# Seven products of quarters for part of the FFN's down projection, and a convolution that reads PSUM

## The chip, the cores and the metric

The kernel runs on one core of a Trainium2 chip. The metric is the device time of one execution in microseconds (us). Before the change the median of three runs is 1321.83 us (1321.08 to 1322.3).

The engines are named as in the profile: PE is TensorE's matmul, PEld its weight load, DVE is VectorE, ACT is ScalarE, POOL is GpSimd, and SP is SyncE, which issues most of the transfers.

## The reference, cut to what matters

The reference is two layers of an encoder on 512 positions of width 1024: a mixer (neighbourhood attention and grouped-query attention), cross attention over 256 memory positions, and a feed-forward network (FFN) with a short convolution. Then a final norm. The change touches the FFN:

```python
def conv_ffn(h, w_up, conv_w, conv_b, w_down):      # D_FF = 2816
    u = h @ w_up                                    # 512 x 1024 by 1024 x 5632
    up = jnp.pad(u, ((0, 0), (1, 1), (0, 0)))
    u = up[:, :-2] * conv_w[0] + up[:, 1:-1] * conv_w[1] + up[:, 2:] * conv_w[2] + conv_b
    gate, val = jnp.split(u, 2, axis=-1)
    return (jax.nn.silu(gate) * val) @ w_down       # 512 x 2816 by 2816 x 1024
```

## The kernel before, in words

**Numbers.** Every float32 operand of a product is split into a part `hi` of type float32r, rounded, and the rest `lo`. A product is then three matmuls, `hi*hi`, `hi*lo` and `lo*hi`, into one PSUM tile (`mm3`, lines 606 to 610). So each operand costs a cast on ACT (`hi`) and a subtraction on DVE or POOL (`lo`). All arrays lie transposed: 128 channels on the partitions, 512 positions along the row. The residual is `xT[0]` to `xT[7]`, one tile for every 128 of the 1024 channels.

**FFN.** D_FF is 22 blocks of 128 channels. For a block `j`, `up_project` (line 1465) makes the gate and the value side, each 8 chunks x 3 = 24 matmuls of 512 columns. `up_finish` (line 1491) multiplies both by the norm's factor `ffn.rep` (DVE, PSUM to an SBUF tile of tag `t`). Then per side ACT makes the middle tap of the convolution, and DVE adds the two outer taps with four `scalar_tensor_tensor`, two of 504 and two of 7 columns (line 1509). Silu, product and split into `hi` and `lo` follow (`acts[j]`, an `rpair`). `down` (line 1517) multiplies a group of blocks by `w_down`: for each of the 8 row blocks `m` of the output one PSUM tile, nj x 3 matmuls of 512 columns, and one DVE addition to `xT[m]`. `GROUPS` holds 8, 7 and 7 blocks. The last group of layer 0 closes the rows for the next norm (`nn.close`). In layer 1 `down_last` (line 1540) computes the first 384 positions as before and the last 128 with the operands swapped, then the final norm and the output.

**Weights.** `weights()` (line 1660) lists the weight blocks in the order of use. `get_w` (line 572) hands out the next one and keeps two more ahead: a DMA into a tile `raw` (`N_RAW` = 2 buffers), a cast on ACT into `hi`, a subtraction on POOL into `lo` (`N_W` = 4 buffers each). A block has up to 1024 columns.

**Order.** Nothing is issued as the code is run. `Tape` records every instruction (hence one line, 393, for nearly all in the profile), and `Tape.plan` orders each engine's list: PE nearly as written, the others by the time at which their results are due. Each engine then works through its own list strictly in order, and semaphores hold it where an operand isn't there. PSUM is eight tiles of 512 columns: 4 of tag `mm`, 2 of `sc`, 2 of `tr` (`ps_mm`, `ps_s`, `ps_t`). In the FFN before, all products go through `mm`.

Of the kernel before, what the change touches and what calls it, by code (L numbers as in the profile page):

```python
# [12 lines left out]
F32R = mybir.dt.float32r  # L13
# [6 lines left out]
P = 128  # L20
S = 512
D = 1024
DEPTH = 2
# [30 lines left out]
MEM_FILL = [1, 1, 2, 2, 1, 3, 1, 3, 1, 3, 1]  # L54
N_ROWS = 3
LATE = 3600
N_RAW, N_W, AHEAD, AHEAD_HELD, N_WARM, N_LATE, N_FIRST = 2, 4, 2, 5, 7, 4, (12, 22)


ENGINES = range(5)  # L60
# [427 lines left out]
def encoder_kernel(ctx: ExitStack, tc: tile.TileContext, t: dict, out: list):  # L488
# [9 lines left out]
    rpool = ctx.enter_context(tc.tile_pool(name="rpool", bufs=21))  # L498
# [24 lines left out]
    def tmp(shape=(S,)):  # L523
        return tpool.tile([P, *shape], F32, tag="t", name=nm("t"))
# [26 lines left out]
    def emit_raw():  # L551
        SP.dma_start(*raw_tile())

    def emit_split(act=ACT, cuts=2):
        n = len(ready)
        key, src, nk, ncol, eng = plan[n]
        raw = raws[n]
        raws[n] = None
        if key[0] in ("up", "down", "memq", "memo"):
# [302 lines left out]
    for l in range(DEPTH):  # L862
# [600 lines left out]
        acts = {}  # L1463

        def up_project(j, side):
            pm = ps_mm()
            gemm_T(pm, get_w(("up", j, side)), ffn.ops, range(KC), 0, KC - 1)
            return pm

        def up_first():  # L1470


            ws, us = [], []
            for side in range(2):
# [7 lines left out]
            us1 = [up_project(1, 0)]  # L1482
            ffn.spread()
            up_finish(0, us)
            us1.append(up_project(1, 1))
            up_finish(1, us1)

        def up(j):
            up_finish(j, [up_project(j, side) for side in range(2)])

        def up_finish(j, us):
            for side in range(2):
                u = tmp()
                DVE.tensor_mul(u, us[side], ffn.rep)
                us[side] = u
            cs = []
            for side in range(2):
                ch = side * NF + j
# [12 lines left out]
            ACT.activation(cs[0], cs[0], AF.Silu)  # L1511
            DVE.tensor_mul(cs[0], cs[0], cs[1])
            acts[j] = rpair()
            ACT.copy(acts[j][0], cs[0])
            DVE.tensor_sub(acts[j][1], cs[0], f(acts[j][0]))

        def down(g):
            j0, nj = GROUPS[g]
# [21 lines left out]
        def down_last(g):  # L1540
# [7 lines left out]
            ws = []  # L1548

            def part(k, c, n):  # L1550
                i, hl = c // 512, ws[3] if k == nj - 1 else ws[k // 2 + 4 * (c // 512)]
                if k == nj - 1:
                    return [w[:, 0, c : c + n] for w in hl]
                return [w[:, k % 2, c - 512 * i : c - 512 * i + n] for w in hl]

            norm = Norm(cols=cs)
            rows = []
            for m in range(KC):
                if m % 4 == 0:
                    ws.extend(get_w(("down", g, n)) for n in range(len(ws), 4 + 3 * (m // 4)))  # L1560
# [59 lines left out]
        for g, (j0, nj) in enumerate(GROUPS):  # L1620
            for j in range(j0 + (g > 0), j0 + nj):
                if j == 0:
                    up_first()
                elif j > 1:
                    up(j)
            if g + 1 < len(GROUPS):
                up(j0 + nj)
            elif l + 1 < DEPTH:
                nn = Norm(G_MIX, l + 1)
            else:  # L1630
                down_last(g)
                break
            down(g)

    tape.play(tc)


# [22 lines left out]
def weights():  # L1660
# [8 lines left out]
    def up(j):  # L1669
        return [cols(("up", j, i), "w_up", 0, KC, i * D_FF + P * j, P) for i in range(2)]  # L1670

    blocks = []
    for l in range(DEPTH):
        for n, p in NA_ORDER:
            if n == "v":
                blocks += wide("v", "w_in", 1024, "DPDP")
            else:
                eng = "Dx" if l == 0 and (n, p) in NA_ORDER[:3] else "P"
                blocks.append(cols((n, p), "w_in", 0, KC, (0 if n == "q" else 512) + P * p, P, eng))
        for kh in range(2):  # L1680
            blocks.append(cols(("gkv", kh), "w_in", 4 * kh, 4, 2048, 256))
        blocks += wide("gq", "w_in", 1536)
        for mp in range(4):
            blocks.append(cols(("outn", mp), "w_out", 0, 4, 256 * mp, 256))
# [11 lines left out]
        for g, (j0, nj) in enumerate(GROUPS):  # L1696
            for j in range(j0 + (g > 0), j0 + nj + (g + 1 < len(GROUPS))):
                blocks += up(j)
            if l + 1 < DEPTH or g + 1 < len(GROUPS):
                blocks += [cols(("down", g, m), "w_down", j0, nj, P * m, P) for m in range(KC)]  # L1700
                continue
            for n, (k0, c0) in enumerate(((0, 0), (2, 0), (4, 0), (6, None), (0, 512), (2, 512), (4, 512))):
                at = (k0, 1, 0, D) if c0 is None else (k0, 2, c0, 512)
                blocks.append(cols(("down", g, n), "w_down", j0 + at[0], *at[1:], "P" if n < 2 else "Pr"))
    return blocks


# [67 lines left out]
```

## Time and profile before

| | |
|---|---|
| median of 3 runs | 1321.83 us |
| the profiled execution: its time | 1320.67 us |
| its span (first to last instruction) | 1318.6 us |
| PE busy | 1311.6 us (99%) |
| DVE / ACT / POOL busy | 939.1 (71%) / 675.6 (51%) / 692.0 us (52%) |
| granted TensorE clock | 1.0 |
| the FFN of layer 0 after its first up block, as one piece of the chain of waits | 315.27 us to 658.11 us |

A busy share counts the time in which the engine has at least one instruction in work. Matmuls overlap: a single one is listed with 390 ns, but the next starts after 227 ns, so times on PE are taken here from start to start. The chain that ended last is followed back from the last instruction; what is on it sets the time. The rows of groups give engine, operation, `out<-in` by tile tags, shape and count, then busy us and mean ns, then the idle time before them.

### The profile page before, as it was taken

To read this page: it belongs to the slowest core of one execution; us is meant where nothing else is said; L and a number is where in the kernel's file an instruction comes from. 1 tells how busy PE (TensorE), PEld (TensorE's weight loads), DVE (VectorE), ACT (ScalarE), POOL (GpSimd) and SP (SyncE) were. 2 spreads that over 40 slices of the span, in tenths; PEclk is the share of its full clock that TensorE was granted. 3 is DMA by queue.
4 is the path that set the end of the run, shared out by engine and by line. 5 is a ranking of instruction groups with operands and counts; after the bars stand their busy time and mean duration, and the time that the engine had idled before them with its cause. 6 is when DMAs were issued, how large, how long until landed. Compare 5 with 4: busy or idle time off the path is not lost.

```text
span 1318.6 us, 17725 instructions
## 1 busy us (share of the span) xinstructions
PE 1311.6 (99%) x6367; PEld 1106.7 (84%) x6367; DVE 939.1 (71%) x1656; ACT 675.6 (51%) x1229; POOL 692.0 (52%) x481
## 2 busy tenths in 40 slices
PE   9999999999999999999999999999999999999998
PEld 8898888888888888888888988888888888888887
DVE  7688886776994488188445898967779835862875
ACT  7786786555442244143447867865644423432432
POOL 3565866726544444444636657765454444444451
PEclk9999999999999999999999999999999999999999
DMA  7752222322333333332355422223133333323331
GB/s 250 208 169 64 82 69 92 96 61 84 112 96 96 97 97 97 102 124 79 101 160 160 145 65 80 69 92 96 49 112 104 99 99 98 92 84 112 96 112 64
DMA packets 42806, 137.28 MB, mean 104 GB/s; under 512 B 5088, under 2 KB 8672, under 8 KB 42720
## 3 DMA queue, kind: packets, MB, share of 16 engines
q1 hardware_dynamic: 42288, 135.83, 33.5%
q8 instruction: 50, 0.82, 0.3%
q10 hardware_dynamic: 432, 0.33, 0.1%
q14 instruction: 36, 0.29, 0.1%
HBM read 126.18 MB, written 2.10 MB: 97 GB/s over the span
## 4 chain that ended last, share of the span: by engine, by line
PE 99%; ACT 0%; DVE 0%; issue 0%; ACTq 0%
PE mm L393 87%; PE sc L393 8%; PE tr L393 4%; ACT t L393 0%; ACT r L393 0%; DVE r L393 0%; DVE s L393 0%; ACTq L393 0%
## 5 line engine op out<-in xcount | busy, mean ns | idle before, releaser
L393 POOL TENSOR_TENSOR lo<-raw,hi 128x1024 fp32r<-128x1024 f32 (+2 forms) x268 | 512.8, 1924 | 490.3 <-ACT hi L393 485.4
L393 PE MATMUL mm<-xg,hi 128*128 128x512 f32 (+1 forms) x1730 | 535.8, 390 | 0.0
L393 ACT CAST hi<-raw 128x512 fp32r<-128x512 f32 (+2 forms) x276 | 226.2, 839 | 355.7 <-PE mm L393 274.7
L393 PEld LDWEIGHTS mm<-xg,hi 128*128 128x128 f32 x1730 | 322.7, 188 | 65.1
L393 PE MATMUL mm<-xg,lo 128*128 128x512 f32 (+1 forms) x865 | 336.8, 389 | 0.0
L393 PE MATMUL mm<-r,hi 128*128 128x512 f32 (+1 forms) x1040 | 326.8, 390 | 0.0
L393 DVE SCALAR_TENSOR_TENSOR t<-t,par,t 128x504 f32<-128x504 f32 (+1 forms) x352 | 286.7, 852 | 38.5 <-ACT t L393 36.5
L393 PEld LDWEIGHTS mm<-r,hi 128*128 128x128 f32 x1040 | 194.4, 188 | 38.6
L393 PE MATMUL mm<-r,lo 128*128 128x512 f32 (+2 forms) x552 | 207.5, 376 | 0.0
L393 PEld LDWEIGHTS mm<-xg,lo 128*128 128x128 f32 x865 | 162.5, 188 | 33.5
L393 PEld LDWEIGHTS mm<-r,lo 128*128 128x128 f32 x552 | 103.7, 188 | 19.3
L393 DVE TENSOR_TENSOR xT<-xT,mm 128x512 f32<-128x512 f32 (+1 forms) x56 | 37.1, 666 | 111.8 <-PE mm L393 111.5
L393 PE MATMUL mm<-hi,xg 128*128 128x512 f32 (+1 forms) x384 | 107.6, 358 | 0.0
L393 POOL TENSOR_SCALAR t<-t,s 128x512 f32<-128x512 f32 (+1 forms) x112 | 66.3, 606 | 65.0 <-DVE s L393 61.2
L393 DVE TENSOR_TENSOR t<-mm,rep 128x512 f32<-128x512 f32 x88 | 60.1, 687 | 36.9 <-PE mm L393 36.8
L393 PE MATMUL sc<-r,r 128*128 128x256 f32 (+1 forms) x382 | 83.5, 336 | 0.0
L393 ACT ACTIVATE t<-t,par 128x512 f32<-128x512 f32 x88 | 71.0, 812 | 18.8 <-DVE t L393 18.8
L393 ACT ACTIVATE t<-sc,s,s 128x512 f32<-128x512 f32 (+1 forms) x96 | 67.9, 711 | 23.7 <-DVE s L393 20.6
L393 PEld LDWEIGHTS mm<-hi,xg 128*128 128x128 f32 x384 | 68.3, 189 | 9.3
L393 PE MATMUL tr<-ident,t 128*128 128x128 f32 x488 | 70.4, 272 | 0.0
L393 PEld LDWEIGHTS tr<-ident,t 128*128 128x128 f32 x488 | 59.3, 140 | 10.8
L393 PE MATMUL mm<-lo,xg 128*128 128x512 f32 (+1 forms) x192 | 68.3, 356 | 0.0
(124 smaller groups left out, 1517.1 us busy)
## 6 DMA issues: line engine op xcount, KB each, us to landing
raw<-in_w SPq DMA_DIRECT2D x192, 512.0 KB, 3.6
raw<-in_w SPq DMA_DIRECT2D x24, 448.0 KB, 3.3
r<-r SPq DMA_DIRECT2D x30, 256.0 KB, 4.0
r<-in_bias SPq DMA_DIRECT2D x16, 384.0 KB, 6.0
r<-in_memT SPq DMA_DIRECT2D x4, 512.0 KB, 7.4
xT<-in_w SPq DMA_DIRECT2D x7, 256.5 KB, 4.2
out<-xT SPq DMA_DIRECT2D x8, 192.0 KB, 2.1
r<-in_w SPq DMA_DIRECT2D x9, 128.0 KB, 3.9
```

The lines of the kernel that those rows point to most:

```text
L393: call(*args, **kwargs)
```

## The change

**Down projection.** Blocks 0 to 15 of D_FF are taken in four groups of four (`GROUPS`), the last six as before. In a group the four blocks are two halves of two. For one pair of row blocks, `m` and `m + 4`, the weights of a group are a 2 x 2 matrix of quarters (rows `m` or `m + 4`, first or second half of the blocks), and the activations are one too (half of the blocks, positions 0 to 255 or 256 to 511). `down_halved` multiplies them by Strassen's scheme in Winograd's form: seven products of quarters for eight, on sums and differences of quarters. Each product has 2 blocks x 3 = 6 matmuls of 256 columns. They go in pairs into the halves of a PSUM tile.

**Sums of weights.** `combined` replaces the split for such a block of 1024 columns: ACT casts 768 and twice 512 columns, DVE subtracts 768, POOL makes four sums of 256 columns and twice subtracts 512. **Sums of activations**: `halved` makes them for two blocks of D_FF at a time. **Order**: `UPS` is the order of the up blocks; from the sixth on, one pair of rows of a group (`BEHIND` = 5) stands behind each up block, in `weights()` and in the loop. **Convolution**: the products of `up_project` go to `sc` and `tr` tiles, the norm's factor is multiplied in place in PSUM, and ACT and DVE read the convolution's input there. `N_RAW` is 3, the pool of `r` tiles has 23 instead of 21 buffers.

The diff, cut:

```diff
-GROUPS = [(0, 8), (8, 7), (15, 7)]
+GROUPS = [(0, 4), (4, 4), (8, 4), (12, 4), (16, 6)]
+UPS = [j0 + i // 2 + nj // 2 * (i % 2) for j0, nj in GROUPS[:-1] for i in range(nj)] + list(range(GROUPS[-1][0], NF))
+BEHIND, ROWS_HALVED = 5, KC // 2 * (len(GROUPS) - 1)
...
+    LO_A, SUMS, LO_S = DVE, POOL, POOL
...
+    def combined(raw):
+        hi, lo = [wpool.tile([P, 6, P], F32R, tag=tag, name=nm(tag)) for tag in ("hi", "lo")]
+        shi, slo = rtile((8, P)), rtile((8, P))
+        a11, a12, a22, a21 = (raw[:, 2 * i : 2 * i + 2] for i in range(4))
+        first, second = tmp((4, P)), tmp((4, P))
+        ACT.copy(hi, raw[:, 0:6])
+        LO_A.tensor_sub(lo, raw[:, 0:6], f(hi))
+        SUMS.tensor_add(first[:, 0:2], a21, a22)
+        SUMS.tensor_sub(first[:, 2:4], a11, a21)
+        SUMS.tensor_sub(second[:, 0:2], first[:, 0:2], a11)
+        SUMS.tensor_sub(second[:, 2:4], a12, second[:, 0:2])
+        for v, c in ((first, slice(0, 4)), (second, slice(4, 8))):
+            ACT.copy(shi[:, c], v)
+            LO_S.tensor_sub(slo[:, c], v, f(shi[:, c]))
...
         def up_project(j, side):
-            pm = ps_mm()
+            pm = ps_t() if side else ps_s()
...
             for side in range(2):
-                u = tmp()
-                DVE.tensor_mul(u, us[side], ffn.rep)
-                us[side] = u
+                DVE.tensor_mul(us[side], us[side], ffn.rep)
...
+        def halved(j, u):
+            n = UPS.index(j)
+            if n % 4 == 0:
+                shared[:] = [rtile((2, 2, H))]
+            if n % 2 == 0:
+                waiting[n + 1] = u
+                hl = shared[0][:, n // 2 % 2]
+                ACT.copy(hl[:, 0], u[:, :H])
+                DVE.tensor_sub(hl[:, 1], u[:, :H], f(hl[:, 0]))
+                return
...
+            DVE.tensor_sub(first[:, 0], a[:, H:], a[:, :H])
+            DVE.tensor_sub(second[:, 0], b[:, 1], first[:, 0])
+            DVE.tensor_sub(first[:, 1], b[:, 1], a[:, H:])
+            DVE.tensor_sub(second[:, 1], b[:, 0], second[:, 0])
+            ACT.copy(bh[:, 0], b)
+            DVE.tensor_sub(bh[:, 1], b, f(bh[:, 0]))
+            for v, c in ((first, slice(0, 2)), (second, slice(2, 4))):
+                ACT.copy(hi[:, c], v)
+                DVE.tensor_sub(lo[:, c], v, f(hi[:, c]))
...
+        def down_halved(g, m):
...
+            def product(pm, a, b):
+                for k, q in enumerate(qs):
+                    mm3(pm, *ws[k // 2][a][k % 2], *q[b], k == 0, k == len(qs) - 1)
...
+            one = pair(("11", "11"), ("s2", "t2"))
+            ACT.copy(u, one[:, :H])
+            DVE.tensor_add(left, left, one[:, :H])
+            DVE.tensor_add(u, one[:, H:], u)
+            two = pair(("12", "21"), ("s4", "22"))
+            DVE.tensor_add(xT[m], xT[m], two)
+            DVE.tensor_add(right, right, u)
+            three = pair(("22", "t4"), ("s1", "t1"))
+            DVE.tensor_add(xT[m + 4], xT[m + 4], three)
+            DVE.tensor_add(right, right, three[:, H:])
+            four = ps_mm()[:, :H]
+            product(four, "s3", "t3")
+            DVE.tensor_add(u, four, u)
+            DVE.tensor_add(below, below, u.unsqueeze(1).to_broadcast([P, 2, H]))
...
+        for n in range(NF):
+            if n == 0:
+                up_first()
+            elif n > 1:
+                up(UPS[n])
+            if 0 <= n - BEHIND < ROWS_HALVED:
+                down_halved(*divmod(n - BEHIND, KC // 2))
```

Two places show the order, each engine's list for itself.

PE, layer 0: before, a row of the down projection in the middle group (`mm_1004` is the PSUM tile of the row, `r_` the activations, `hi_992` and `lo_993` the weights):

```order
L393 MATMUL mm_1000<-r_986,hi_988 128x512 x2
L393 MATMUL mm_1000<-r_986,lo_989 128x512
L393 MATMUL mm_1004<-r_876,hi_992 128x512 x2
L393 MATMUL mm_1004<-r_876,lo_993 128x512
L393 MATMUL mm_1004<-r_921,hi_992 128x512 x2
L393 MATMUL mm_1004<-r_921,lo_993 128x512
L393 MATMUL mm_1004<-r_934,hi_992 128x512 x2
```

PE after the change, layer 0: the last matmul of an up block (tag `tr`, value side), and the first of the rows behind it (`mm_846` holds the products `one`):

```order
L395 MATMUL tr_831<-xg_641,lo_818 128x512
L395 MATMUL mm_846<-r_775,hi_824 128x256 x2
L395 MATMUL mm_846<-r_775,lo_825 128x256
L395 MATMUL mm_846<-r_775,hi_824 128x256 x2
L395 MATMUL mm_846<-r_775,lo_825 128x256
L395 MATMUL mm_846<-r_785,r_826 128x256
```

The matmuls of 512 columns of the down projection have become ones of 256, each with its own weights, and they stand between up blocks instead of in one piece behind a group.

DVE, layer 0, before: one up block (`t_846` and `t_847` are the two sides in SBUF, `t_848` and `t_849` the convolution's sums):

```order
L393 TENSOR_TENSOR t_846<-mm_838,rep_770 128x512
L393 SCALAR_TENSOR_TENSOR t_836<-t_834,par,t_836 128x504
L393 SCALAR_TENSOR_TENSOR t_836<-t_834,par,t_836 128x7
L393 TENSOR_TENSOR t_835<-t_835,t_836 128x512
L393 SCALAR_TENSOR_TENSOR t_848<-t_846,par,t_848 128x504
L393 SCALAR_TENSOR_TENSOR t_848<-t_846,par,t_848 128x7
L393 TENSOR_TENSOR t_847<-mm_842,rep_770 128x512
L393 TENSOR_TENSOR r_837<-t_835,r_837 128x512
```

DVE after the change, layer 0, an up block of the value side (`tr_880`) up to the additions of the next rows (`mm_918` holds their products `one`; `lo_924` is the subtraction of a weight block):

```order
L395 SCALAR_TENSOR_TENSOR t_885<-tr_880,par,t_885 128x7
L395 TENSOR_TENSOR t_884<-t_884,t_885 128x512
L395 TENSOR_TENSOR t_888<-t_884,t_887 128x256
L395 TENSOR_TENSOR t_887<-t_884,t_862 128x256
L395 TENSOR_TENSOR t_888<-t_884,t_888 128x256
L395 TENSOR_TENSOR r_886<-t_884,r_886 128x512
L395 TENSOR_TENSOR lo_924<-raw_906,hi_923 128x768
L395 TENSOR_TENSOR r_890<-t_887,r_889 128x512
L395 TENSOR_TENSOR r_890<-t_888,r_889 128x512
L395 TENSOR_TENSOR xT_79<-xT_79,mm_918 128x256
L395 TENSOR_TENSOR t_917<-mm_918,t_917 128x256
```

The convolution's input is now a PSUM tile, and eight operations with two SBUF inputs stand in one row, ahead of additions that wait for PE.

More of the change, by code (lines that the diff above doesn't have):

```diff
@@ L552, in emit_raw @@
         SP.dma_start(*raw_tile())
+    def combined(raw):
[12 more added lines that the diff above has]
+            LO_S.tensor_sub(slo[:, c], v, f(shi[:, c]))
+        parts = {}
+        for i, n in enumerate(("11", "12", "22")):
+            parts[n] = [(hi[:, 2 * i + k], lo[:, 2 * i + k]) for k in range(2)]
+        for i, n in enumerate(("s1", "s3", "s2", "s4")):
+            parts[n] = [(shi[:, 2 * i + k], slo[:, 2 * i + k]) for k in range(2)]
+        return parts
     def emit_split(act=ACT, cuts=2):
@@ L558, in emit_split @@
         raws[n] = None
+        if eng == "S":
+            ready.append(combined(raw))
+            return
         if key[0] in ("up", "down", "memq", "memo"):
@@ L1512, in up_finish @@
             DVE.tensor_mul(cs[0], cs[0], cs[1])
+            if j < GROUPS[-1][0]:
+                halved(j, cs[0])
+                return
             acts[j] = rpair()
@@ new lines, in down_halved, with pair @@
+        def down_halved(g, m):
+            j0, nj = GROUPS[g]
+            qs = [quads[j] for j in range(j0, j0 + nj // 2)]
+            ws = [get_w(("down", g, m, q)) for q in range(nj // 4)]
+            def product(pm, a, b):
+                for k, q in enumerate(qs):
+                    mm3(pm, *ws[k // 2][a][k % 2], *q[b], k == 0, k == len(qs) - 1)
+            def pair(left, right):
+                pm = ps_mm()
+                product(pm[:, :H], *left)
+                product(pm[:, H:], *right)
+                return pm
+            left, right = (xT[m][:, c] for c in (slice(0, H), slice(H, S)))
+            below = xT[m + 4].rearrange("p (n q) -> p n q", n=2)
+            u = tmp((H,))
+            one = pair(("11", "11"), ("s2", "t2"))
[12 more added lines that the diff above has]
+            DVE.tensor_add(below, below, u.unsqueeze(1).to_broadcast([P, 2, H]))
@@ L1550, in part @@
             def part(k, c, n):
-                i, hl = c // 512, ws[3] if k == nj - 1 else ws[k // 2 + 4 * (c // 512)]
-                if k == nj - 1:
-                    return [w[:, 0, c : c + n] for w in hl]
+                i, hl = c // 512, ws[k // 2 + 3 * (c // 512)]
                 return [w[:, k % 2, c - 512 * i : c - 512 * i + n] for w in hl]
@@ L1559, in down_last @@
                 if m % 4 == 0:
-                    ws.extend(get_w(("down", g, n)) for n in range(len(ws), 4 + 3 * (m // 4)))
+                    ws.extend(get_w(("down", g, n)) for n in range(len(ws), 3 + 3 * (m // 4)))
                 rows.append(ps_mm()[:, :N_COLS])
@@ L1618, in down_last @@
             ACT.dma_start(out[1][:, 640:D], yf[:, 640:])
[L1620 to L1633, printed above, removed]
+        for n in range(NF):
[5 more added lines that the diff above has]
+                down_halved(*divmod(n - BEHIND, KC // 2))
+        if l + 1 < DEPTH:
+            nn = Norm(G_MIX, l + 1)
+            down(len(GROUPS) - 1)
+        else:
+            down_last(len(GROUPS) - 1)
     tape.play(tc)
@@ L1670, in up, with quarters @@
         return [cols(("up", j, i), "w_up", 0, KC, i * D_FF + P * j, P) for i in range(2)]
+    def quarters(key, k0, half, m):
+        k = np.array([k0, k0 + 1])
+        ks = np.concatenate([k, k + half, k + half, k])
+        rows = (ks[:, None] * P + np.arange(P)).T
+        return key, "w_down", l, rows, np.repeat([P * m, P * (m + 4)], 4), P, "S"
     blocks = []
@@ L1695, in weights @@
             blocks.append(cols(("memo", 0, mp), "w_mem_o", 0, 4, 256 * mp, 256))
[L1696 to L1704, printed above, removed]
+        for n in range(NF):
+            blocks += up(UPS[n])
+            if 0 <= n - BEHIND < ROWS_HALVED:
+                g, m = divmod(n - BEHIND, KC // 2)
+                j0, nj = GROUPS[g]
+                blocks += [quarters(("down", g, m, q), j0 + 2 * q, nj // 2, m) for q in range(nj // 4)]
+        g = len(GROUPS) - 1
+        j0, nj = GROUPS[g]
+        if l + 1 < DEPTH:
+            blocks += [cols(("down", g, m), "w_down", j0, nj, P * m, P) for m in range(KC)]
+            continue
+        for n in range(6):
+            blocks.append(cols(("down", g, n), "w_down", j0 + 2 * (n % 3), 2, 512 * (n // 3), 512, "P" if n < 2 else "Pr"))
     return blocks
@@ L1755 @@
     a["w_in"] = a["w_in"][:, :, _in_order()]
-    blocks = [a[name][l, rows][:, :, c0 : c0 + ncol] for _, name, l, rows, c0, ncol, _ in weights()]
+    blocks = [
+        a[name][l, rows][:, :, c0 : c0 + ncol] if np.ndim(c0) == 0 else
+        np.stack([a[name][l, rows[:, i], c : c + ncol] for i, c in enumerate(c0)], axis=1)
+        for _, name, l, rows, c0, ncol, _ in weights()]
     x = np.concatenate([a["x"].reshape(ROWS, GW, D).transpose(2, 1, 0).reshape(D, S), a["norm_mix"][0][:, None]], axis=1)
```

21 lines of the change are left out of this document (16 added, 5 removed).

## The prediction

> **What bounds the kernel now.** I read the page's busy times first, then the chain of waits, then the FFN's stretches by window, and last the groups of DVE and POOL there.
>
> The page's busy times, and its shares of the chain that ended last by engine:
>
> ```profile
> PE 1311.6 (99%) x6367; PEld 1106.7 (84%) x6367; DVE 939.1 (71%) x1656; ACT 675.6 (51%) x1229; POOL 692.0 (52%) x481
> PE 99%; ACT 0%; DVE 0%; issue 0%; ACTq 0%
> ```
>
> The chain of waits in order of time (start, length, what, count):
>
> ```profile
> 94.65 3.36 PE mm L393 x28
> ...
> 315.27 342.84 PE mm L393 x1512
> ...
> 967.26 333.92 PE mm L393 x1512
> ```
>
> PE carries the end, and in the FFN it has no gap at all: one piece of 1512 matmuls in layer 0, another in layer 1. So matmul time taken out of the FFN comes off the end, as long as that piece stays whole. 342.84 us / 1512 = 226.7 ns is what a matmul of 512 columns costs. For 256 and 384 columns the timeline has stretches of one kind (a merged row starts with its first matmul):
>
> ```profile
> 94.97 0.28 PE L393 MATMUL mm<-hi,xg 128*128 128x256 f32 x1
> ...
> 97.73 0.29 PE L393 MATMUL mm<-hi,xg 128*128 128x256 f32 x1
> ...
> 1295.81 5.37 PE L393 MATMUL mm<-r,r 128*128 128x384 f32 x30
> ```
>
> From 94.97 to 97.73 us the timeline holds 23 starts, so 256 columns cost 2.76 / 23 = 120 ns; the chain's 3.36 / 28 says the same. Each of them loads its own weights, as the new products do. For 384 columns the 30 starts end one tail (0.33 us less a pitch) before the row's end: about 174 ns.
>
> **PE: removed and added.** Blocks 0 to 15 cost, in layer 0, 8 rows x 16 x 3 = 384 matmuls of 512 columns. In layer 1 one of the sixteen stood in the last group, so there it is 8 x 15 x 3 = 360 of 512 columns, 24 of 384 and 6 of 512 with swapped operands. Removed: 750 x 226.7 + 24 x 174 = 170.0 + 4.2 = 174.2 us. Added: 2 layers x 16 row pairs x 7 products x 6 = 1344 matmuls, x 120 = 161.3 us. Seven products for eight would take off an eighth, 21 us; as 256 columns cost more than half of 512, 12.9 us stay. All of it lies in the unbroken pieces.
>
> Here a page speaks against the change. The Trainium skill, "TensorE: Matmul & The Clock Gate", section "Back-to-back issue gap", gives streams of weight load and matmul about 131 ns at 512 columns and 81 at 128; on a straight line between, an estimate of 98 at 256, the sum would be a loss of some 31 us. This trace disagrees at both sizes (226.7 and 120 ns), so the rows decide.
>
> **DVE in the FFN.** This is what could break the cover. A stretch of up blocks alone, then one of down rows alone, before (columns: length, then busy us of PE, PEld, DVE, ACT, POOL):
>
> ```profile
> 446.00:518.00 72.00, 72.00 (x319) 59.64 (x318) 59.59 (x78) 30.35 (x40) 31.93 (x14) 1.00 0.30 95
> 403.00:441.00 38.00, 38.00 (x169) 31.50 (x168) 11.11 (x14) 8.45 (x10) 17.26 (x7) 1.00 0.31 96
> ```
>
> An up block is 48 x 226.7 ns = 10.88 us of PE, and DVE is busy 83% of it, 9.00 us; POOL 4.83 us. The down rows, where DVE rests, are now mixed in: a step after the change is an up block and a row pair, 10.88 + 42 x 0.120 = 15.92 us. Its DVE work, from the groups of the FFN of layer 0 (316 to 667 us), and two smaller ones from the whole run:
>
> ```profile
> L393 DVE SCALAR_TENSOR_TENSOR t<-t,par,t 128x504 f32<-128x504 f32 x88 | 117.4, 1339 | 19.6 <-ACT t L393 18.6
> L393 DVE TENSOR_TENSOR t<-mm,rep 128x512 f32<-128x512 f32 x44 | 30.1, 687 | 17.7 <-PE mm L393 17.7
> L393 DVE TENSOR_TENSOR xT<-xT,mm 128x512 f32<-128x512 f32 x16 | 11.0, 688 | 51.6 <-PE mm L393 51.5
> L393 DVE SCALAR_TENSOR_TENSOR xg<-mm,par,xg 128x512 fp32r<-128x512 f32 x8 | 6.0, 748 | 5.1 <-ACT xg L393 5.1
> L393 DVE TENSOR_TENSOR r<-t,r 128x512 fp32r<-128x512 f32 x22 | 26.1, 1184 | 3.0 <-ACT r L393 2.2 <-DMA raw<-in_w 0.7
> ...
> L393 DVE TENSOR_TENSOR t<-mm,r 128x256 f32<-128x256 f32 x16 | 6.0, 420 | 1.3 <-ACT t L393 1.2
> ```
>
> The first and the fifth row stand out: with both inputs in SBUF an operation takes 1339 or 1184 ns, with one in PSUM 748 or 688. The timeline of one up block shows why:
>
> ```profile
> 461.73 0.74 DVE L393 SCALAR_TENSOR_TENSOR t<-t,par,t 128x504 f32<-128x504 f32 x1
> 462.39 0.68 DVE L393 TENSOR_TENSOR t<-mm,rep 128x512 f32<-128x512 f32 x1
> 463.00 0.22 DVE L393 SCALAR_TENSOR_TENSOR t<-t,par,t 128x7 f32<-128x7 f32 x1
> ...
> 469.37 2.47 DVE L393 SCALAR_TENSOR_TENSOR t<-t,par,t 128x504 f32<-128x504 f32 x1 [0.33 <-ACT t L393]
> 471.77 0.68 DVE L393 TENSOR_TENSOR r<-t,r 128x512 fp32r<-128x512 f32 x1
> ```
>
> POOL's row of that moment:
>
> ```profile
> 468.70 2.60 POOL L393 TENSOR_TENSOR lo<-raw,hi 128x1024 fp32r<-128x1024 f32 x1 [3.04 <-ACT hi L393]
> ```
>
> Undisturbed, the 504 columns take 0.74 us from SBUF as well; with a POOL operation running they end only after it (471.30), at 2.47. Two PSUM-fed rows at the same stretch don't stretch at all. So the convolution from PSUM costs the same work and loses the waits. "The exclusive lock" of two-input DVE operations and POOL's stands in the Trainium skill, "SBUF — State Buffer", section "Who interferes with whom", and this trace agrees (2.47 against 0.74 us). "VectorE: DVE Perf Modes", section "Rules for kernel authors", would instead copy PSUM to SBUF ahead of many operations; here the rows speak for PSUM.
>
> Neighbours overlap: 461.73, 462.39, 463.00 are 0.66 and 0.61 us apart, so 0.08 less than listed. On that scale a step costs DVE: two factors 1.22, four long taps 2.64, four short 0.56 (0.22 less 0.08), the product 0.61; half a pair of `halved` (five of 256 columns at 0.34, three of 512 at 0.61, halved) 1.77; `combined`'s 768 columns 0.88 (straight line through 0.42 and 0.69); the row pair (five of 256, three of 512) 3.53. Together 11.2 us of 15.92. Of these 0.61 + 1.77 + 0.88 + 0.95 = 4.2 us, 38%, have both inputs in SBUF; before it was 4.4 of 5.6, 78%.
>
> POOL's prices over the whole run, and ACT's from the FFN:
>
> ```profile
> L393 POOL TENSOR_TENSOR lo<-raw,hi 128x1024 fp32r<-128x1024 f32 x122 | 303.5, 2493 | 330.4 <-ACT hi L393 330.4
> L393 POOL TENSOR_TENSOR lo<-raw,hi 128x512 fp32r<-128x512 f32 x122 | 156.9, 1304 | 90.6 <-ACT hi L393 88.9 <-POOL t L393 1.0 <-PE mm L393 0.8
> ...
> L393 POOL TENSOR_TENSOR t<-t,s 128x256 f32<-128x256 f32 x4 | 2.4, 613 | 0.0
> ...
> L393 ACT CAST hi<-raw 128x1024 fp32r<-128x1024 f32 x46 | 48.4, 1052 | 127.3 <-PE mm L393 106.2 <-issue 19.0 <-POOL lo L393 2.1
> ```
>
> On POOL a step has two of the first, two of the second and four of the third: 5.0 + 2.6 + 2.4 = 10.0 us, 63%, and room. ACT was busy 30.35 of 72 us, 4.6 per up block; `combined` adds 1792 columns and `halved` 384, some 2.2 us by the cast's row, and a copy: under 8 us of 15.92, clear. The transfers are the same bytes.
>
> What is open is how much DVE waits for POOL. Before, 9.00 - 5.64 = 3.4 us per up block, 70% of POOL's 4.83. Bounds after: nothing, or again 70% of 10.0 = 7.0 us. I take it in proportion to the share of two-SBUF operations, 70 x 38 / 78 = 34%, so 3.4 us: 14.6 of 15.92. PE stays ahead. DVE's in-order list also hides a lag: an `sc` tile is asked for again a full step after its last reader's place, about 15.9 us.
>
> **Ends.** The last group has six blocks, so what covers the last up block's convolution is three rows x 5 x 3 x 0.2267 = 10.2 us instead of 12.2. Before, the last block of layer 0 took this on DVE:
>
> ```profile
> 620.07 0.69 DVE L393 TENSOR_TENSOR t<-mm,rep 128x512 f32<-128x512 f32 x1 [0.22 <-PE mm L393]
> ...
> 626.73 0.69 DVE L393 TENSOR_TENSOR r<-t,r 128x512 fp32r<-128x512 f32 x1 [0.69 <-ACT r L393]
> ```
>
> From PE's end to the split that is 7.6 us, with waits for POOL in it that go; I cost it at nothing, with 2.6 us in hand. In the tail, PE closes 3 x 0.227 us earlier after the last norm, but output transfers queue there:
>
> ```profile
> 1310.61 3.83 SPq L393 DMA_DIRECT2D out<-xT  x8
> ...
> 1314.61 0.33 SPq L393 DMA_DIRECT2D out<-r  x1
> ```
>
> SP is free at 1314.44, so only 0.2 of the 0.7 us comes through: +0.5.
>
> **Sum.** -12.9 + 0.5 = -12.4 us. The profiled execution took 1320.67 (span 1318.6), so 1308.3; on the median, 1.2 higher, 1309.4 us.
>
> **Rivals.**
> *DVE becomes the bound (slower).* Should DVE lose 70% of POOL's time again, a step costs it 18.2 us, 2.3 over PE's. Over 16 steps that is 37 us per layer, less the 15.9 of lag: 21 per layer, 42 in all: 1351 us. It starts to cost at 4.7 + 1.0 = 5.7 us of waits per step (57% of POOL's time) and turns the sign at 61%. For it: eight two-SBUF operations stand in one row of the new order, so POOL operations can slip between. Against: nearly half the DVE work can't be held. Chance 0.15; a loss that just cancels the gain, 1319.2 to 1324.5: 0.06.
> *A wait takes a part back.* The six-block cover is too short, or the first `sc` and `tr` tiles, which wait for the norm, come free late: 2 us per layer, the cover lost, to 4, with a wait for one POOL operation of 2.5 us on top: 1313 to 1318. For: block 0's factor comes late. Against: the piece in the chain is whole from 315.27 on. Chance 0.10.
> *Weights set the pace at 256 columns.* Were each held for a whole listed load, 1344 x 188 ns:
>
> ```profile
> L393 PEld LDWEIGHTS mm<-hi,xg 128*128 128x128 f32 x384 | 68.3, 189 | 9.3
> ```
>
> that is 253 against 174.2 removed, so 1400 us; the stretch at 120 ns has such loads, so 0.01. (The page's issue gap, with its +31 us, is in this 0.01.)
>
> **Numbers.** Forecast: 0.68, from 1306 to 1312 (1 ns on 1344 pitches is 1.3 us). A measurement of this kernel tells 0.2%, 2.6 us, from no change. Faster 0.68 + 0.10 = 0.78, same 0.06, slower 0.16. The range goes from 1305.5 (below: three ns less per new matmul) to 1323, leaving out the DVE rival and little else.
>
> **What would show it.** Right: 1344 matmuls of 256 columns 120 ns apart, the FFN of each layer one PE piece in the chain, some 6 us shorter; long taps near 750 ns; DVE 90% busy in the steps, POOL 65 to 75%. Wrong: PE idle before `sc`, `tr` or `mm` tiles released by DVE, DVE at 99% with two-SBUF operations far over 1 us, or a pitch above 125 ns.

## The result, and the profile after

| | before | after |
|---|---|---|
| median, beside each other on one chip | 1321.45 us (4 runs, 1320.64 to 1322.3) | 1311.41 us (4 runs, 1309.79 to 1311.78) |
| profiled execution: time, span | 1320.67, 1318.6 us | 1311.38, 1309.5 us |

The ratio is 0.9922, with a 95% interval of 0.9904 to 0.9939: 10 us faster, where 12.4 were forecast. The changed kernel was timed twice more, unaltered: 1311.77 us (1310.3 to 1313.7, ratio 0.9923, 0.9911 to 0.9936) and 1312.31 us (1310.32 to 1313.78, ratio 0.9929, 0.9917 to 0.9942).

The page after, busy times and the chain's shares by engine:

```profile
PE 1300.4 (99%) x6937; PEld 1121.5 (86%) x6937; DVE 1088.9 (83%) x2008; ACT 723.8 (55%) x1356; POOL 824.6 (63%) x640
PE 95%; DVE 1%; DMA 1%; POOL 0%; SPq 0%; ACT 0%; issue 0%; POOLq 0%; ACTq 0%
```

PE holds the end as before. It has 570 matmuls more and is busy 11.2 us less. In the FFN the chain of waits goes through PE alone; its pieces now carry the names of three tiles (`sc` and `tr` for an up block, `mm` for a row pair). A step of layer 0 and the start of the next, and the last group's rows in layer 1:

```profile
419.50 5.47 PE sc L395 x24
424.97 5.44 PE tr L395 x24
430.41 5.03 PE mm L395 x42
435.44 5.47 PE sc L395 x24
...
1267.75 24.99 PE mm L395 x144
```

A step is 435.44 - 419.50 = 15.94 us, where 15.92 was forecast, and 42 products of 256 columns take 5.03 us: 120 ns each. The steps follow each other without a gap, and the last rows (24.99 us for 144) are one piece, so the cover held. Eight steps of each layer, by window (columns as before):

```profile
419.50:547.02 127.52, 127.52 (x722) 112.36 (x721) 118.28 (x190) 56.99 (x87) 90.65 (x63) 1.00 0.33 100
1033.69:1161.21 127.52, 127.52 (x721) 112.36 (x721) 122.85 (x192) 57.86 (x88) 92.00 (x63) 1.00 0.33 100
```

DVE is busy 118.28 / 8 = 14.8 us of a step in layer 0 and 15.4 in layer 1, 93 and 96%: the reserve is 1.1 and 0.6 us. POOL is busy 71%. DVE's groups in the first of these windows show where the waits went:

```profile
L395 DVE TENSOR_TENSOR xT<-xT,t 128x256 f32<-128x256 f32 x8 | 12.3, 1538 | 0.0
L395 DVE SCALAR_TENSOR_TENSOR t<-tr,par,t 128x504 f32<-128x504 f32 x16 | 11.8, 737 | 1.6 <-ACT t L395 1.3
L395 DVE SCALAR_TENSOR_TENSOR t<-sc,par,t 128x504 f32<-128x504 f32 x16 | 11.7, 734 | 0.0
L395 DVE TENSOR_TENSOR lo<-raw,hi 128x768 fp32r<-128x768 f32 x7 | 10.8, 1539 | 0.0
...
L395 DVE TENSOR_TENSOR r<-t,r 128x256 fp32r<-128x256 f32 x4 | 6.4, 1611 | 2.3 <-ACT r L395 2.3
```

The long taps went from 1339 to 735 ns. Some of what still reads two SBUF tiles is held long: 256 columns that cost 0.42 us undisturbed take 1.54 and 1.61. It depends on where an operation stands, for other such rows of the same window are at 0.61 (256 columns, `t<-t,t`) and 0.78 (512 columns, `r<-t,r`, 1.18 before).

To see where the 9.1 us of span came from, PE's small matmuls behind each norm serve as marks. The second norms' in both layers and the last norm's, before:

```profile
314.98 0.29 PE L393 MATMUL tr<-s,sel 128*128 128x16 f32 x2
669.10 0.29 PE L393 MATMUL tr<-s,sel 128*128 128x16 f32 x2
966.97 0.29 PE L393 MATMUL tr<-s,sel 128*128 128x16 f32 x2
1308.56 0.28 PE L393 MATMUL tr<-s,sel 128*128 128x12 f32 x2
```

The same four after:

```profile
317.27 0.29 PE L395 MATMUL tr<-s,sel 128*128 128x16 f32 x2
665.33 0.29 PE L395 MATMUL tr<-s,sel 128*128 128x16 f32 x2
963.34 0.29 PE L395 MATMUL tr<-s,sel 128*128 128x16 f32 x2
1299.45 0.28 PE L395 MATMUL tr<-s,sel 128*128 128x12 f32 x2
```

| stage | before | after | difference |
|---|---|---|---|
| up to the FFN of layer 0 | 314.98 | 317.27 | +2.3 |
| FFN of layer 0 | 354.12 | 348.06 | -6.1 |
| between the FFNs | 297.87 | 298.01 | +0.1 |
| FFN of layer 1 | 341.59 | 336.11 | -5.5 |
| from there to the span's end | 10.04 | 10.05 | 0.0 |

The last row hides two parts, PE's 0.7 us less and a tail that gives it back. After, the queues' issues there are these:

```profile
1301.50 3.85 SPq L395 DMA_DIRECT2D out<-xT  x8
...
1305.44 0.41 SPq L395 DMA_DIRECT2D out<-r  x1
```

SP is free at 1301.50 + 3.85 = 1305.35, and the last output goes out there; the other one, on ACT's queue, left at 1305.07. Whether that queue sets the end is asked below. The FFN gave what the sum said. What the sum didn't have are 2.3 us ahead of the first FFN, where the diff touches no instruction, only two counts of buffers (raw weight blocks and `r` tiles).

### The profile page after: what moved, and what is told of

Same layout as the page of the kernel before. It is cut to its first block, busy times and chain, and to the rows that moved or that the text cites. A ratio compares the mean times of both kernels' runs of the same rounds, so it can differ in the third digit from the quotient of the medians.

```text
span 1309.5 us, 19611 instructions
## 1 busy us (share of the span) xinstructions
PE 1300.4 (99%) x6937; PEld 1121.5 (86%) x6937; DVE 1088.9 (83%) x2008; ACT 723.8 (55%) x1356; POOL 824.6 (63%) x640
## 4 chain that ended last, share of the span: by engine, by line
PE 95%; DVE 1%; DMA 1%; POOL 0%; SPq 0%; ACT 0%; issue 0%; POOLq 0%; ACTq 0%
PE mm L395 50%; PE sc L395 24%; PE tr L395 22%; DMA raw<-in_w 1%; SPq L395 0%; DVE r L395 0%; DMA r<-in_w 0%; DVE t L395 0%; DVE lo L395 0%; DVE s L395 0%; POOL lo L395 0%; POOL xT L395 0%; ACT r L395 0%; DVE sc L395 0%; ACT hi L395 0%
## 5 line engine op out<-in xcount | busy, mean ns | idle before, releaser
L395 POOL TENSOR_TENSOR lo<-raw,hi 128x512 fp32r<-128x512 f32 (+2 forms) x236 | 437.7, 1866 | 297.6 <-ACT hi L395 295.4
L395 PE MATMUL mm<-r,hi 128*128 128x512 f32 (+2 forms) x928 | 248.3, 346 | 0.0
L395 PE MATMUL sc<-xg,hi 128*128 128x512 f32 (+1 forms) x740 | 229.1, 391 | 0.0
L395 PE MATMUL tr<-xg,hi 128*128 128x512 f32 x672 | 207.1, 389 | 0.0
L395 PE MATMUL mm<-r,lo 128*128 128x256 f32 (+2 forms) x496 | 165.9, 334 | 0.0
L395 PEld LDWEIGHTS sc<-xg,hi 128*128 128x128 f32 x740 | 137.1, 189 | 27.1 <-ACT hi L395 0.4
L395 PE MATMUL mm<-r,r 128*128 128x256 f32 (+2 forms) x1040 | 158.1, 293 | 0.0
L395 PEld LDWEIGHTS mm<-r,r 128*128 128x128 f32 x1040 | 142.3, 191 | 2.6 <-DVE r L395 0.2
L395 PE MATMUL sc<-xg,lo 128*128 128x512 f32 (+1 forms) x370 | 143.4, 389 | 0.0
L395 PE MATMUL mm<-xg,hi 128*128 128x512 f32 (+1 forms) x386 | 120.8, 393 | 0.0
L395 DVE TENSOR_TENSOR r<-t,r 128x512 fp32r<-128x512 f32 (+1 forms) x84 | 93.5, 1138 | 11.3 <-ACT r L395 11.2
```

The source lines that it names most:

```text
L395: call(*args, **kwargs)
```

## The experiments

My theory: PE's cut in matmul time is the gain, and it holds because the convolution reads PSUM; without that, DVE would wait for POOL and PE for DVE. The rivals: the taps' place is indifferent; the cut in columns costs more or less than the pitch says; the spreading of the rows is unnecessary; the sums belong on DVE.

**The convolution from PSUM alone (kernel before).** The products go to the `sc` and `tr` tiles, and the factor is multiplied in place; nothing else is changed.

```diff
-            pm = ps_mm()
+            pm = ps_t() if side else ps_s()
...
-                u = tmp()
-                DVE.tensor_mul(u, us[side], ffn.rep)
-                us[side] = u
+                DVE.tensor_mul(us[side], us[side], ffn.rep)
```

> The kernel before with the convolution reading PSUM (products in sc and tr tiles), nothing else of the change. Theory: PE sets the time, so 1320 to 1323 us, no change; but DVE's busy time falls by about 2.5 us per up block, some 100 us over the run, long taps from 1343 to 740 ns. Rival: the earlier convolution itself shortens something on the path: below 1318 us.

Measured: 1320.69 us (ratio 0.9994, 0.9985 to 1.0003): no change. The window of up blocks that the prediction read, and the taps in it:

```profile
446.00:518.00 72.00, 72.00 (x320) 59.62 (x319) 40.28 (x78) 31.02 (x41) 30.81 (x14) 1.00 0.31 96
```

```profile
L393 DVE SCALAR_TENSOR_TENSOR t<-sc,par,t 128x504 f32<-128x504 f32 x14 | 10.4, 743 | 5.7 <-ACT t L393 5.5
```

DVE's busy time falls from 59.59 to 40.28 us for the same 78 instructions, and POOL's stays at 31. So a third of DVE's time in an up block was waiting, and PSUM as the source takes it away. On the time it does nothing as long as PE is the bound. The Trainium skill, "SBUF — State Buffer", section "Who interferes with whom", says that a DVE instruction with at most one SBUF input, outside the two-port modes, does not contend with GpSimd; the 743 ns beside a POOL that works as much as before agree.

**The cut in columns alone (kernel before).** The down products of the first two groups are made as two halves of 256 columns, without the scheme: 720 matmuls more, the same arithmetic.

```diff
-                    gemm_T(pm, get_w(("down", g, m)), ops, range(nj), 0, nj - 1)
...
+                        for c in (slice(0, S // 2), slice(S // 2, S)):
+                            for k in range(nj):
+                                mm3(pm[:, c], wh[:, k], wl[:, k], ops[k][0][:, c], ops[k][1][:, c], k == 0, k == nj - 1)
```

> The kernel before with every matmul of the first two groups of the down projection (360 of 512 columns in each layer) cut into two of 256, nothing saved. Theory: a matmul of 256 columns costs 120 ns against 113.4, half of 226.7. 720 times 13.3 ns is 9.6 us slower than before, 1331 us, with PE still in one piece. Rival: small matmuls cost more than that where the operands come from other places, 130 ns or over: 1345 us; or the halves cost nothing extra: 1321 us.

Measured: 1330.71 us (ratio 1.0071, 1.0057 to 1.0084). The chain's pieces of the FFN:

```profile
315.81 347.68 PE mm L393 x1872
...
972.63 338.76 PE mm L393 x1872
```

Against 342.84 and 333.92 us they are 9.7 us longer, for 720 x (2 x 120 - 226.7) = 9.6 us. The price of the cut stands. The scheme's 1344 half products pay it 672 times, 8.9 us, and it takes that from the eighth.

**The convolution back in SBUF (changed kernel).**

```diff
-                DVE.tensor_mul(us[side], us[side], ffn.rep)
+                u = tmp()
+                DVE.tensor_mul(u, us[side], ffn.rep)
+                us[side] = u
```

> The changed kernel with the convolution's input copied to SBUF again (products still in sc and tr tiles). Theory: DVE operations with two SBUF inputs wait for POOL. Two-SBUF share of DVE's work in a step goes from 38% to 66%, the waits from 3.6 to some 5.9 us per step, DVE needs 17.1 us for a step of 15.94, and after a lag of one step PE waits: 3 us per layer, so 1316 to 1322 us, long taps near 1300 ns. Rival: PE alone sets the time, the convolution's place is indifferent: 1310 to 1312 us, FFN step 15.94.

Measured: 1340.63 us (ratio 1.0144, 1.013 to 1.0158): the sign was right, the size was not. Eight steps, and the taps in them:

```profile
420.00:548.00 128.00, 126.78 (x704) 109.73 (x703) 126.12 (x182) 56.59 (x84) 94.48 (x61) 1.00 0.32 94
```

```profile
L395 DVE SCALAR_TENSOR_TENSOR t<-t,par,t 128x504 f32<-128x504 f32 x28 | 29.5, 1074 | 0.0
```

The taps are at 1074 ns, DVE is busy 98.5%, and PE does 704 matmuls where the changed kernel does 722 in half a us less. From mark to mark the FFNs are 357.8 and 353.9 us long, 9.8 and 17.8 more than after the change. The sixteen steps with a row pair lose about the same in both layers, 7.8 and 7.3 us (262.7 and 262.6 us from the first row pair's first matmul to the last group's, against 254.9 and 255.3 in the changed kernel); the rest is lost at the last group's rows. In layer 1 PE waits ahead of them. PE's first matmul there, and the DVE operation that ends the wait:

```profile
1294.83 0.98 PE L395 MATMUL mm<-r,hi 128*128 128x384 f32 x2 [8.46 <-DVE t L395]
```

```profile
1294.27 0.41 DVE L395 TENSOR_TENSOR t<-mm,t 128x256 f32<-128x256 f32 x1
```

The DVE operation reads the first `mm` tile of the last row pair, which PE had filled by 1272. The last group's rows need that tile, and in DVE's list the addition stands behind the convolutions of the last up blocks. After the wait the granted clock is low for a while, which takes another 1.6 us (here and in all windows of PE alone: length, busy, granted clock, DMA share, GB/s):

```profile
1294.83:1298.50 3.67, 3.67 (x13) 0.56 0.00 0
```

In layer 0 DVE is behind as well, but there PE starts the last group's rows at once, and they take 34.74 us instead of 32.64. I had credited DVE with a lag of one step per layer, 15.9 us, that costs nothing. That was too much. By its count of instructions (182 in 128 us, against 190 in eight steps of the changed kernel) a step costs DVE an estimated 16.7 us, so it needs 12 us more than PE over the sixteen steps; that is less than the credit, and yet PE loses 7 to 8 us in them. And layer 1 shows that a lag can fall due at the end of the FFN, though layer 0 pays little for it.

**The sums on DVE (changed kernel).** POOL keeps the splits of the up weights alone.

```diff
-    LO_A, SUMS, LO_S = DVE, POOL, POOL
+    LO_A, SUMS, LO_S = DVE, DVE, DVE
```

> The changed kernel with POOL's part of a combined weight block (four sums, two subtractions) moved to DVE. Theory: a step's own DVE work grows from 11.2 to 13.8 us, POOL's falls from 10.0 to 5.0, DVE's waits are then about 44% of 5.0, 2.2 us: 16.0 us for a step of 15.94. DVE is busy all the time, close to the point from which it sets the time. Since the second experiment showed that a lag of DVE is not forgiven but paid at the end of the FFN, a loss of 1 to 6 us: 1312 to 1318 us. Rival, that POOL's use of the port is the cost and not DVE's sum: DVE gets as much back in waits as it takes in work, 1309 to 1312 us.

Measured: 1339.09 us (ratio 1.0131, 1.0117 to 1.0145), far above what I expected. The steps of the first six row pairs of layer 0, and of the next six:

```profile
364.47:460.91 96.44, 96.38 (x541) 84.30 (x539) 93.66 (x159) 40.84 (x61) 30.43 (x12) 1.00 0.28 91
460.91:565.33 104.42, 99.04 (x541) 85.14 (x541) 102.18 (x182) 43.74 (x66) 29.17 (x12) 1.00 0.30 91
```

The groups of POOL and DVE from 420 to 548 us:

```profile
L395 POOL TENSOR_TENSOR lo<-raw,hi 128x1024 fp32r<-128x1024 f32 x15 | 36.4, 2427 | 91.2 <-ACT hi L395 91.2
...
L395 DVE TENSOR_TENSOR t<-t,raw 128x256 f32<-128x256 f32 x7 | 8.5, 1220 | 0.0
L395 DVE TENSOR_TENSOR lo<-raw,hi 128x768 fp32r<-128x768 f32 x7 | 8.1, 1160 | 0.0
```

In the second window a step is 104.42 / 6 = 17.4 us and DVE is busy 17.0 us of it, 98%: it has become the bound. Its own work is an estimated 11.2 us a step and the moved sums (four of 256 columns at 0.34, two of 512 at 0.61): 13.8. So it waits some 3.2 us, 66% of the 4.86 that POOL is still busy with, where I had taken 44%. POOL's work was more than halved, and the waits hardly fell: in the changed kernel they were 3.6 us a step in layer 0 and 4.2 in layer 1. Two POOL operations of 2.4 us a step still find a two-SBUF operation of DVE nearly each time. That sums of 256 columns beside them take 1.2 us on average and not 0.42 is the same wait.

The first window shows what a lag is worth. Six steps take 96.4 us, only 0.8 more than in the changed kernel, so DVE could fall some 8 us behind (six times 17.4 less 16.1, an estimate) before PE was held. In layer 0 this lag was not paid later either: the last group's rows run in one piece of 32.64 us, as in the changed kernel. In all the FFNs became 13.4 and 16.1 us longer.

**The rows of a group in one piece (changed kernel).** Four row pairs stand behind each fourth up block; before, one stood behind each.

```diff
-            if 0 <= n - BEHIND < ROWS_HALVED:
-                down_halved(*divmod(n - BEHIND, KC // 2))
+            if 0 <= n - BEHIND < ROWS_HALVED and (n - BEHIND) % 4 == 0:
+                for m in range(KC // 2):
+                    down_halved((n - BEHIND) // 4, m)
...
```

The part that is not shown puts the weights into the same order.

> The changed kernel with the four row pairs of a group in one piece, behind up blocks 5, 9, 13 and 17, instead of one behind each up block. Same instructions. Theory: what keeps PE whole is that DVE and POOL get 15.94 us for every row pair; in one piece four pairs take PE 20.2 us and need about 20 us of POOL work and, with waits, over 20 us of DVE, so PE waits for weights or for PSUM: 2 to 5 us per piece, eight pieces, 1327 to 1350 us. Rival: the number of matmuls alone counts and the place does not matter: 1309 to 1313 us.

Measured: 1335.32 us (ratio 1.0103, 1.0088 to 1.0119). One such piece, in the timeline of PE:

```profile
441.86 0.63 PE L395 MATMUL sc<-xg,hi 128*128 128x512 f32 x2
444.72 0.50 PE L395 MATMUL mm<-r,hi 128*128 128x256 f32 x2 [2.23 <-DVE t L395]
```

DVE's list at that place:

```profile
442.33 0.21 DVE L395 SCALAR_TENSOR_TENSOR t<-sc,par,t 128x7 f32<-128x7 f32 x1
...
442.60 0.68 DVE L395 TENSOR_TENSOR xT<-xT,mm 128x512 f32<-128x512 f32 x1
...
444.25 0.42 DVE L395 TENSOR_TENSOR t<-mm,t 128x256 f32<-128x256 f32 x1
```

PE has filled its `mm` tiles and waits until the addition at 444.25 has read one; ahead of the additions DVE's list has a whole convolution (442.33 is the last tap of its `sc` side). A row pair gives DVE 3.5 us of additions and sums for 5.04 of PE, and four of them in a row leave no time for the convolution between. So the spreading carries its part as well: the same operations in another order cost 24 us. What PE loses there is in most pieces more than the wait; that is told at the end.

**The tail (changed kernel, two raw buffers).** Two of the eight output transfers go to ACT's queue, so that SP is free earlier.

```diff
-                SP.dma_start(out[0][k * P : (k + 1) * P, :], xk)
+                (ACT if k in (2, 5) else SP).dma_start(out[0][k * P : (k + 1) * P, :], xk)
```

> The changed kernel with two raw buffers, as in the first experiment, and two of the eight output transfers of the final norm issued by ACT instead of SP. Theory: SP's queue of eight issues (3.85 us) holds the last output transfer for about 0.7 us; with six it is free in time and the end comes 0.3 to 0.7 us sooner, 1310 us, and the time from the last matmul to the end falls from 7.3 to 6.6 to 7.0 us. Rival: the issues on ACT delay its last two operations by as much, no change from the first experiment (1310.6).

Measured: 1310.58 us (ratio 0.9915, 0.9901 to 0.9928), the same as with two raw buffers alone (1310.58, below). SP's last issue with eight outputs on its queue (two raw buffers alone), and with six:

```profile
1304.20 0.40 SPq L395 DMA_DIRECT2D out<-r  x1
```

```profile
1303.73 0.44 SPq L395 DMA_DIRECT2D out<-r  x1
```

Counted from the last norm's mark (1298.23 and 1298.11 us), the last output leaves after 5.97 us and after 5.62. So SP's queue did hold it, and now it doesn't. But from the mark to the span's end it is 10.1 us in both. The rival's reason is not what the trace shows: ACT's last operation starts 4.98 us after the mark in both. The transfer itself takes longer, 3.4 us from its issue to its landing instead of 3.0. Five us of each tail show why, beginning 1 us after the first output's issue: the kernel before, the changed kernel, two raw buffers alone, and this kernel (columns as before, the last two DMA share and GB/s):

```profile
1311.61:1316.61 5.00, 0.74 (x4) 0.28 (x2) 2.19 (x5) 1.30 (x3) 1.95 (x3) 1.00 1.03 376
```

```profile
1302.50:1307.50 5.00, 0.06 (x1) 0.00 (x0) 2.19 (x5) 1.30 (x3) 1.90 (x3) 0.86 1.02 374
```

```profile
1301.28:1306.28 5.00, 0.00 (x0) 0.00 (x0) 2.11 (x5) 1.23 (x3) 1.90 (x3) 0.90 1.03 374
```

```profile
1301.16:1306.16 5.00, 0.00 (x0) 0.00 (x0) 2.10 (x5) 1.24 (x3) 1.90 (x3) 0.70 1.03 373
```

The DMA engines are fully busy in all four, whichever queue issues. The output has 1024 x 512 x 4 bytes, 2.1 MB, which is 5.6 us at 374 GB/s, and the end comes 8.0 us after the first output's issue in all four. So the transfers of the output set the tail, and neither SP's queue nor PE's last matmuls do. The queue is not worth an edit.

**The third raw buffer.** Of the two counts, it is the one that lets weights be fetched earlier at the start. Five runs bear on it. The changed kernel with two buffers:

```diff
-N_RAW, N_W, AHEAD, AHEAD_HELD, N_WARM, N_LATE, N_FIRST = 3, 4, 2, 5, 7, 4, (12, 22)
+N_RAW, N_W, AHEAD, AHEAD_HELD, N_WARM, N_LATE, N_FIRST = 2, 4, 2, 5, 7, 4, (12, 22)
```

> The changed kernel with two raw weight buffers again (N_RAW 3 back to 2). Theory: the FFN kept the whole predicted saving (12.9 us) and the 2.3 us that the first mixer lost come from the third buffer, whose early transfers stand ahead of others at the start. Then the second reduction of the first FFN's norm (317.3 us after, 315.0 before) comes back to about 315, the FFN step stays 15.94 us, and the kernel takes 1309 us. Rival: the loss comes from the whole order being planned anew, not from the buffer. Then the first mixer ends anywhere within 2 us of before, and the time is 1310 to 1313. Should the row pairs need the third buffer, the FFN step grows and the time goes over 1313.

Measured: 1310.58 us (1310.19 to 1310.84; ratio 0.9917, 0.9903 to 0.993), with the first FFN's mark at 315.58. Its interval overlaps that of the changed kernel, so a second run of the changed kernel, unaltered, bears on it:

> The changed kernel once more, unaltered, beside the others on one chip: 1311.4 us, first mixer's second reduction at 317 us. If the first experiment's 0.8 us are real, this is slower than the kernel with two raw buffers by 0.5 to 1 us; if not, within 0.3.

Measured: 1311.77 us, the mark at 316.21. Then three kernels side by side: the kernel before with three buffers, the two-buffer kernel again, the changed kernel again.

> The kernel before with three buffers for raw weight blocks instead of two, nothing else. Theory one: the third buffer by itself lets a third weight block's transfer start in the first 30 us and compete with the inputs that the first mixer waits for; then the FFN's first matmul (the end of the second norm reduction) comes 1 to 2 us later than the 315.0 to 315.5 us of the kernel before, and the time is 1 to 2 us above it (1322 to 1324). Rival: the first mixer's end depends on the order of the rest of the program or differs from run to run by itself; then it stays at 315.0 to 315.5 and the time within 0.5 us of the kernel before.

> The changed kernel with two buffers for raw weight blocks, once more, beside the next run. Theory one (the third buffer delays the first mixer): second norm reduction ends at 315 to 316 us, time 1310 to 1311, some 1 us below the run beside it. Rival (differs from run to run): no difference to the run beside it beyond 0.3 us, and first mixers that overlap.

> The changed kernel unaltered, a third time. Theory one: second norm reduction at 316 to 318 us and 1311.4 to 1312 us, as in its first two runs. Rival: at 315 to 316 us in this run, 1310.5.

Measured: the kernel before with three buffers 1321.67 us (ratio 1.0, 0.9991 to 1.0009), its mark at 315.21. The changed kernel with two buffers 1310.78 us (1310.26 to 1311.29; ratio 0.992, 0.9906 to 0.9933), with three 1312.31. In the changed program the marks do not overlap: 315.12, 315.25 and 315.58 with two buffers (the tail's run among them), 316.21, 316.92 and 317.27 with three. Neither do the runs spread alike: nine times with two buffers alone lie in 1310.19 to 1311.29 (median 1310.58), fourteen with three in 1309.79 to 1313.78 (median 1311.65). So the third buffer costs about 1 us, and two buffers are the better version by that. The mark does not tell all of it. The second run of the changed kernel reached it at 316.21 us and its profiled execution still took 1310.3 us, as short as those with two buffers; between the FFNs it needed 298.0 us, they 298.6. The third run (1313.4 us) lost another 1.2 us within the first FFN and 1.1 between the FFNs. Why is not settled. It does let weights come earlier; the windows from 20 to 30 us, two buffers and then three:

```profile
20.00:30.00 10.00, 10.00 (x48) 8.30 (x47) 7.51 (x15) 4.08 (x7) 6.63 (x6) 1.00 0.58 207
```

```profile
20.00:30.00 10.00, 10.00 (x46) 8.04 (x45) 7.47 (x12) 6.19 (x11) 9.84 (x9) 1.00 0.86 306
```

The DMA share is 0.58 against 0.86. But the second row is the kernel before with three buffers, which loses nothing by it. And the edited kernels above, with three buffers too, reached their mark at 315.3 (sums on DVE), 315.8 (rows in one piece) and 318.2 (taps in SBUF). So earlier transfers by themselves don't delay the mixer; the order into which they fall must matter as well, and which instruction pays was not found. The count of `r` tiles was not tried by itself.

## Why the prediction was right, point by point

- **PE's sum (-12.9).** Right in mechanism and nearly in size: 6.1 + 5.5 + 0.7 (the last behind the last norm) = 12.3 us of matmul time; the 0.7 of it does not reach the end, as the tail shows. The step measured 15.94 instead of 15.92 us, which over 32 steps is the missing 0.6.
- **256 columns at 120 ns.** Shown twice, by 5.03 us for 42 and by the cut alone, 9.7 us for 720.
- **DVE stays behind PE.** Right, but with less room than I gave it: 14.8 and 15.4 us of a step, not 14.6. Its own work of 11.2 us is an estimate that no run shows alone. With it the waits are 14.8 - 11.2 = 3.6 and 15.4 - 11.2 = 4.2 us. POOL was busy 11.3 and 11.5 us of a step, not 10.0, so this is 32 and 37% of it, where 34% was taken. The number fits, but the rule behind it does not hold, as the next point but one says; that it fits here is partly luck.
- **PSUM-fed rows are not held by POOL.** The conclusion was right, the rows read for it showed nothing. The PSUM-fed operations near that place start at 462.39, 467.75 and 473.28 us and last 0.7 us; POOL works from 463.26 to 465.66, from 468.70 to 471.30 and again from 474.14, so none of them met it. The kernel with the convolution from PSUM alone showed it, with its 743 ns.
- **The rival in which DVE becomes the bound** was real: with the taps in SBUF, or the sums on DVE, it happened. Two of its steps were wrong. The credit of 15.9 us of lag per layer was too high: with the sums on DVE PE was held once DVE was some 8 us behind, and with the taps in SBUF one of two layers paid for the lag at the end. With a credit of nothing to 8 us, PE begins to lose at 4.7 to 5.2 us of waits per step, 42 to 46% of POOL's 11.3, not at 5.7; the changed kernel was at 4.2 in layer 1, nearer than I thought. And the waits are not in proportion to the share of two-SBUF operations: they went from 70% of POOL's busy time before to 32 to 37% after, but stood at 66% with POOL's work halved.
- **The tail (+0.5).** It gave back 0.7, but not by the mechanism named. The last output does stand behind SP's queue, yet with the queue free the end came no sooner: the output's transfers keep the DMA engines full. That the number came close is luck.
- **The rivals with a short cover or late tiles** did not occur: the pieces in the chain are whole.
- **What the sum lacked:** 2.3 us ahead of the first FFN. I read the third raw buffer as part of the FFN's supply and never asked what it does at the start of the program. It accounts for some 1 to 1.5 us of them by the two-buffer runs; the rest is within what one profile differs from the next (0.5 us between the marks of the runs with two buffers).

## What to carry to other kernels

A scheme that saves an eighth of the products and halves their columns must be costed with the pitch of the narrow product: here the cut took 9 us of the 21. When an engine in order is fed by one that is nearly full, price its work per step with its waits, and credit a lag only as far as a run shows it: here PE was held when DVE was some 8 us behind, and in one layer the lag came due at the end of the stage. And an operation's source can matter more than its size: moving the taps' input from SBUF to PSUM was worth nothing alone, and 29 us once DVE had no reserve.

## What the runs showed of the hardware

A short wait of PE can cost more than itself. In the kernel with the rows in one piece, PE alone, by window, in the wait of 2.23 us of layer 0, behind it, and further on:

```profile
441.90:444.60 2.70, 0.59 (x4) 1.00 0.50 185
444.70:448.40 3.70, 3.68 (x18) 0.56 0.00 0
448.50:452.50 4.00, 4.00 (x35) 1.00 0.14 31
```

Behind it the granted clock is 0.56 for 3.7 us, in which PE does half the matmuls of a like stretch: another 1.6 us. The next piece shows the same (0.63 for 3.68 us after a wait of 2.22). Layer 1 has two waits of 2.23 us at the same place of the program, and behind them:

```profile
1105.12:1108.82 3.70, 3.70 (x30) 1.00 0.00 0
1171.33:1175.03 3.70, 3.70 (x20) 0.61 0.01 2
```

So three of four such waits were followed by a low clock and one was not; what decides is not shown. The stretch is no longer after the wait of 8.46 us in the kernel with the taps in SBUF (0.56 for 3.67 us, 1.00 behind it). In the kernel with the sums on DVE, shorter waits left the clock as it was; one of them in PE's timeline, and the window behind it:

```profile
500.80 0.50 PE L395 MATMUL mm<-r,hi 128*128 128x256 f32 x2 [1.25 <-DVE xT L395]
```

```profile
503.50:507.50 4.00, 3.98 (x17) 1.00 0.15 8
```

After 1.25 us of waiting the clock is at 1.00. The Trainium skill, "TensorE: Matmul & The Clock Gate", section "What's actually happening", puts the slow state behind at least one idle window of about 3.4 us; the slow stretch of 3.7 us here is about that long, but the waits that led to it were 2.2 us in three cases.
